# The first two query blocks of a head done at one point of the attention: 24 points in place of 32, in a decoder layer on one Trainium2 core

## The chip, the core and the metric

One core of a Trainium2 chip runs the whole layer in one launch. The metric is the device time of that launch in microseconds: the median of 3 runs of the kernel before is 610.11 us (609.85 to 610.28). The core has a matmul engine (PE, with PEld for its weight loads), a vector engine (DVE), a scalar engine (ACT), GpSimd (POOL) and SyncE (SP), each with its own list of instructions which it works off in order; they wait for each other by semaphores only. Most DMAs are issued from SP, the accumulating ones from POOL.

## The reference

One layer over 512 tokens of width 1024. A combined projection gives nine pieces of 1024 columns; two mixers, a gated MLP (branch A) and a differential attention (branch B), are merged and projected again, with a per-layer embedding and a LayerNorm at the end. The part that the change touches is the attention: 8 heads, two softmax maps each over 64-wide queries and keys, values of 128 columns.

```
h = x @ w_in
ua, va, za, qh, kh, vh, zb, ga, gb = jnp.split(h, IN_OFFSETS, axis=-1)
...
def block(args):                      # 128 queries, causal
    sc = jnp.einsum("bqhmd,bkhmd->bhmqk", qblk, k)
    sc = jnp.where(mask, sc, -jnp.inf)
    pr = jax.nn.softmax(sc, axis=-1)
    a = pr[:, :, 0] - lam * pr[:, :, 1]
    return jnp.einsum("bhqk,bkhd->bqhd", a.astype(v.dtype), v)
...
o = rms_norm(o, b_subln_g[i]) * (1.0 - lam_init)
yb = o.reshape(bn, s_len, B_WIDTH) * jax.nn.silu(zb)
```

## The kernel before, in words

All large products are done as three matmuls of a high and a low part (`three`, L279), each a 128x512 matmul; such a matmul is called a product here. Every product goes through `product` (L267), which counts it in `clock[0]` and then calls whatever has been put on an agenda with `later(n, fn)` for that count. So all side work is placed by hand, in units of products: it is written into the engines' lists between two products, and that decides the order on every engine. The matmuls that the side work itself issues are not counted.

The attention lies inside the stage that projects k, q, ua (three rounds of 144 products, `rope` and `ua_pair`) and za (192 products). Its softmax runs while these products run. For a head h and a block i of 128 queries (32 pairs in all) there are four steps, placed by `block` (L860) at points given by the table `starts`:

- `scores` (L763) at `starts[e]`, e = 4h+i: four matmuls of 128 queries by n = 128(i+1) keys into two `sc` banks of PSUM (L769), then on DVE the mask with a running minimum (L776), a small correction (L780), and on ACT the exponential with its sum (L782), once for each map.
- `combine` (L786) `COMBINE[i]` products later, on DVE: reciprocal, ratio, and the two maps joined (L790, L792, L794).
- `transposes` (L798) at `starts[e + 2]`: i+1 transposes on PE into the only `tr` bank, and one ACT copy out of it (`at`, L805).
- `values` (L808) at `starts[e + 3]`: i+1 matmuls into the head's `po` bank (L814), of which there is one.

At one point of `starts`, PE therefore gets values of block e-3, transposes of block e-2 and scores of block e, in this order, between two products. A head's four blocks start 13, 16, 20 and 23 products apart (`PERIOD`, L50; for the last two heads times 0.78), 72 products a head.

After a head's last values come `squares` (L818: DVE multiplies `po` into `on`, L823, and clamps it; ACT squares it), `norm` (L830: DVE sums, POOL takes the power, L840, L841), `scale` (POOL, L847), `gated` (DVE, L851) and `turned` (L853: four transposes of `on` on PE, L857, and an ACT copy). `TAIL` and `LAST_TAIL` give their distances in products from the last values. `on` has one buffer, `at` two (shared with the squares), `p0`/`p1` three, q, k and kx three each.

Of the weights, each 128x1024 unit (24 products) is split by ACT (`wh`, L389) and DVE (`wl`, L392) about three units before it is used, on the same lists as the attention's side work. `wr` buffers are asked for again by SP once `wl` is made.

Of the kernel before, what the change touches and what calls it, by code (L numbers as in the profile page):

```python
# [17 lines left out]
AF = mybir.ActivationFunctionType  # L18
OP = mybir.AluOpType
AX = mybir.AxisListType  # L20

P = 128
D = 1024
T = 512
KT = D // P
NT = T // P
NH = 8
DK = 64
# [18 lines left out]
SWAP = 290  # L47
BEGIN = 14
STRETCH = 0.78
PERIOD = (13, 16, 20, 23)  # L50
COMBINE = (10, 11, 13, 12)
LAST_TURNS = (14, 27, 45)
PAIR = 144
TAIL = (2, 14, 26, 44, 56)
LAST_TAIL = (2, 10, 20, 32, 42)
SILU = (122, 5)
NORM = (174, 224, 276, 326)
SPLITS = {'va': ((0, 10), (13, 16)), 'wb': ((4, 7), (13, 16)), '': ((0, 4), (6, 12))}
# [175 lines left out]
def hybrid_layer(ctx: ExitStack, tc: tile.TileContext, a, out: bass.AP):  # L234
    nc = tc.nc
    pe, dve, act, pool, sp = nc.tensor, nc.vector, nc.scalar, nc.gpsimd, nc.sync
# [9 lines left out]
    def pbank(tag, bufs):  # L246
        return psum.tile([P, T], F32, tag=tag, name=f"ps_{tag}", bufs=bufs)
# [150 lines left out]
    def next_unit(name):  # L398
        u = cursor[0]
        assert STEPS[u][0] == name, (STEPS[u][0], name)  # L400
        cursor[0] += 1
        for g in (prep(u), prep(u + 1), prep(u + 2)):
            run(g)
        if not pumping:
            for v in range(u + 3, u + 6):
                run(load(v))
        spread(u + 3)
        if name in EARLY_ASK:
            later(ASK, lambda: run(load(u + 6)))
        return split.pop(u)  # L410
# [67 lines left out]
    ident = consts.tile([P, P], F32, name="ident")  # L478
# [6 lines left out]
    mask = ap_.tile([P, T], F32, name="mask")  # L485
# [8 lines left out]
    cs = rp.tile([P, T], F32, name="cs")  # L494
# [87 lines left out]
    neglam = consts.tile([P, 1], F32, name="neglam")  # L582
# [44 lines left out]
    def quad(name, left, banks, place, done):  # L627
# [132 lines left out]

    todo = {}

    def scores(h, i):  # L763
        n = (i + 1) * P
        q, k0, k1 = stacks["q", h], stacks["k", h], stacks["kx", h]
        sc = [pbank("sc", 2) for _ in range(2)]
        for m in range(2):
            for o, kk in enumerate((k0, k1)):
                pe.matmul(sc[m][:, :n], q[:, m, i * P:(i + 1) * P], kk[:, m, :n],  # L769
                          start=o == 0, stop=o == 1)  # L770
        pr = [ap_.tile([P, T], F32, name=f"p{m}", tag=f"p{m}", bufs=3) for m in range(2)]
        if i == 0:
            todo["st", h] = small([P, NT, 4], "sth", 2)
        st = todo["st", h][:, i, :]
        for m in range(2):
            dve.tensor_tensor_reduce(out=pr[m][:, :n], in0=sc[m][:, :n], in1=mask[:, T - n:],  # L776
                                     scale=-(DK ** -0.5), scalar=3e38, op0=OP.add, op1=OP.min,
                                     accum_out=st[:, m:m + 1])
            if m == 0:
                dve.tensor_scalar(out=st[:, 0:1], in0=st[:, 0:1], scalar1=-math.log(T),  # L780
                                  scalar2=None, op0=OP.add)
            act.activation(pr[m][:, :n], pr[m][:, :n], AF.Exp, bias=st[:, m:m + 1], scale=-1.0,  # L782
                           accum_out=st[:, 2 + m:3 + m])
        todo[h, i] = pr, st

    def combine(h, i):  # L786
        n = (i + 1) * P
        pr, st = todo[h, i]
        r1 = small([P, 1], "r1")
        dve.reciprocal(out=r1, in_=st[:, 3:4])  # L790
        rho = small([P, 1], "rho")
        dve.tensor_scalar(out=rho, in0=r1, scalar1=st[:, 2:3], scalar2=neglam[:, 0:1],  # L792
                          op0=OP.mult, op1=OP.mult)
        dve.scalar_tensor_tensor(out=pr[0][:, :n], in0=pr[1][:, :n], scalar=rho[:, 0:1],  # L794
                                 in1=pr[0][:, :n], op0=OP.mult, op1=OP.add)
        todo[h, i] = pr[0]

    def transposes(h, i):  # L798
        n = (i + 1) * P
        ad = todo[h, i]  # L800
        tr = pbank("tr", 1)
        for j in range(i + 1):
            pe.transpose(tr[:, j * P:(j + 1) * P], ad[:, j * P:(j + 1) * P], ident)  # L803
        at = ap_.tile([P, T], F32, name="at", tag="at", bufs=2)
        act.activation(at[:, :n], tr[:, :n], AF.Copy)  # L805
        todo[h, i] = at

    def values(h, i):  # L808
        at = todo.pop((h, i))
        if i == 0:  # L810
            todo["po", h] = pbank("po", 1)
        po = todo["po", h]
        for j in range(i + 1):
            pe.matmul(po[:, i * P:(i + 1) * P], at[:, j * P:(j + 1) * P],  # L814
                      v[:, j, h * P:(h + 1) * P], start=j == 0, stop=j == i)


    def squares(h):  # L818
        po = todo.pop(("po", h))
# [37 lines left out]
            pe.transpose(tr[:, i * P:(i + 1) * P], on[:, i, :], ident)  # L857
        act.activation(yb[:, h, :], tr, AF.Copy, scale=g08[:, 0:1])

    def block(h, i, starts):  # L860
        e = NT * h + i
        later(starts[e], scores, h, i)
        later(starts[e] + COMBINE[i], combine, h, i)
        later(starts[e + 2], transposes, h, i)
        later(starts[e + 3], values, h, i)
        if i == NT - 1:
            tail = TAIL if h < 5 else LAST_TAIL
            for d, fn in zip(tail, (squares, norm, scale, gated)):
                later(starts[e + 3] + d, fn, h)

    def attention():
        starts = []
        for h in range(NH):
            stretch = 1.0 if h < NH - 2 else STRETCH
            at = PAIR * (h // 2) + BEGIN + h % 2 * sum(PERIOD) * stretch
            for n in PERIOD:
                starts.append(round(at))
                at += n * stretch
        starts += [starts[-1] + n for n in LAST_TURNS]
        for h in range(NH):  # L880
            for i in range(NT):
                block(h, i, starts)
        for h in range(NH - 1):
            later(starts[NT * h + 9], turned, h)
        later(starts[-1] + LAST_TAIL[4], turned, NH - 1)

    later(LAMBDAS[0], load_constants)
    for n, fn in zip(LAMBDAS[1:], (lam_dots, lam_exps, lam)):
# [57 lines left out]
    for k in range(KT):  # L946
        if k % 2 == 0:
            h, l = next_unit("kq")
# [423 lines left out]
    for those in ((0, 1), (2, 3)):  # L1372
        for k in range(KT):
# [9 lines left out]
            h, l = units[k // 2]  # L1383
            m = slice((k % 2) * T, (k % 2 + 1) * T)
# [9 lines left out]
    for t in range(NT):  # L1394
        ts = slice(t * P, (t + 1) * P)
        for i, (c0, c1) in enumerate(last_columns[t][1:], 1):
            for k in range(KT):
# [4 lines left out]
                h, l = units[k // 2]  # L1402
                m = slice((k % 2) * T + c0 - T, (k % 2) * T + c1 - T)
# [45 lines left out]
```

## Time and profile before

| | |
|---|---|
| median of 3 runs | 610.11 us (609.85 to 610.28) |
| the profiled execution | 610.13 us, of which the span from first to last instruction is 608.2 us |
| PE busy | 600.1 us, 99% of the span, 2880 records |
| PEld / DVE / ACT / POOL busy | 503.1 / 464.8 / 346.7 / 125.4 us |
| attention stage | about 117 to 307 us of the span |
| PE / DVE / ACT / POOL busy in 117 to 307 us | 190.0 / 154.2 / 112.2 / 56.9 us |
| granted TensorE clock | 0.997 over the span |

How to read it: times are us from the start of the span. A row of the timeline gives start, duration, engine, line of the kernel, operation, what it writes and reads, and a count where equal rows were merged; in brackets the idle time before it and what ended that. A matmul's end is modelled and overlaps the next one's start, so on PE the distance from one start to the next says what a matmul costs, not the duration shown. A row of the groups gives busy time, mean ns of one, and idle time before. L numbers are lines of the kernel before.

### The profile page before, as it was taken

What the parts mean: (1) busy time and instruction counts of PE and PEld (TensorE: products, weight loads), DVE (VectorE), ACT (ScalarE), POOL (GpSimd) and SP (SyncE); (2) the same over time, 40 slices, a digit from 0 to 9 for tenths busy, and PEclk for the clock granted to TensorE, in tenths of its full rate; (3) what the DMA queues carried; (4) which work ended last, traced back from release to release, by engine and by line L of the source; (5) the groups of instructions that cost most, each with busy time, mean ns of one, the idle gap of its engine ahead of it and who ended that gap; (6) DMA issues with size and microseconds to landing.
All of it is one profiled execution on the core that took longest, in us unless ns stands there. A gap on an engine that the chain in (4) does not pass through costs nothing.

```text
span 608.2 us, 8270 instructions
## 1 busy us (share of the span) xinstructions
PE 600.1 (99%) x2880; PEld 503.1 (83%) x2880; DVE 464.8 (76%) x770; ACT 346.7 (57%) x537; POOL 125.4 (21%) x133
## 2 busy tenths in 40 slices
PE   9999999999999999999999999999999999999995
PEld 6888888888888888888888888888888888888885
DVE  6995645588789789678965788779687887879476
ACT  6656475755745745746676666554776565555310
POOL 1234121041252432422110321331120011110011
PEclk9999999999999999999999999999999999999998
DMA  8689899697887896892579988976999578997002
GB/s 309 228 246 182 252 205 227 237 240 252 277 208 277 273 258 230 240 313 61 150 310 288 305 241 217 273 175 191 286 244 306 172 206 250 253 256 288 27 35 103
DMA packets 44541, 138.23 MB, mean 227 GB/s; under 512 B 5940, under 2 KB 7092, under 8 KB 44148
## 3 DMA queue, kind: packets, MB, share of 16 engines
q1 hardware_dynamic: 34436, 102.97, 46.8%
q0 software_dynamic: 9488, 34.35, 30.6%
q8 instruction: 22, 0.36, 0.2%
q10 hardware_dynamic: 576, 0.39, 0.2%
q14 instruction: 19, 0.16, 0.1%
HBM read 118.69 MB, written 29.49 MB: 244 GB/s over the span
## 4 chain that ended last, share of the span: by engine, by line
PE 98%; DVE 1%; DMA 0%; DVEq 0%; issue 0%
PE ps_pp L268 56%; PE ps_sc L268 22%; PE ps_tx L268 9%; PE ps_sc L769 3%; PE ps_po L814 3%; PE ps_tr L803 1%; PE ps_po L268 1%; PE ps_tr L268 1%; PE ps_tr L1133 1%; PE ps_po L1133 1%; PE ps_tx L857 1%; DMA xr<-in_xT 0%; PE ps_po L1319 0%; PE ps_tr L1319 0%; DVE base L1361 0%; DVE xl L295 0%
## 5 line engine op out<-in xcount | busy, mean ns | idle before, releaser
L392 DVE TENSOR_TENSOR wl<-wr,wh 128x1024 fp32r<-128x1024 f32 x133 | 165.4, 1250 | 36.7 <-ACT wh L389 36.5
L389 ACT ACTIVATE wh<-wr 128x1024 fp32r<-128x1024 f32 x133 | 139.4, 1054 | 68.7 <-PE ps_pp L268 20.5
L268 PE MATMUL ps_pp<-xh,wh 128*128 128x512 f32 x232 | 91.2, 394 | 0.0
L268 PE MATMUL ps_pp<-xh,wl 128*128 128x512 f32 x232 | 91.0, 393 | 0.0
L268 PE MATMUL ps_pp<-xl,wh 128*128 128x512 f32 x232 | 90.4, 391 | 0.1
L365 POOL DMA_DIRECT2D wr<-in_w x30 | 25.8, 872 | 153.6 <-DVE wl L392 150.6
L268 PE MATMUL ps_pp<-wl,xh 128*128 128x512 f32 (+1 forms) x148 | 56.9, 384 | 0.0
L268 PE MATMUL ps_pp<-wh,xl 128*128 128x512 f32 (+1 forms) x148 | 56.8, 384 | 0.0
L268 PE MATMUL ps_pp<-wh,xh 128*128 128x512 f32 (+1 forms) x148 | 56.7, 383 | 0.0
L782 ACT ACTIVATE p<-p,sth 128x128 f32<-128x128 f32 (+3 forms) x64 | 35.5, 556 | 28.2 <-DVE sth L780 28.0
L268 PEld LDWEIGHTS ps_pp<-xl,wh 128*128 128x128 f32 x232 | 43.6, 188 | 9.3 <-DVE xl L295 0.5
L268 PEld LDWEIGHTS ps_pp<-xh,wh 128*128 128x128 f32 x232 | 43.5, 188 | 9.0 <-ACT wh L294 0.6
L268 PEld LDWEIGHTS ps_pp<-xh,wl 128*128 128x128 f32 x232 | 43.6, 188 | 8.7
L776 DVE CUSTOM_DVE_ANT_0 p<-ps_sc,mask 128x128 f32<-128x128 f32 (+3 forms) x64 | 31.0, 484 | 19.3 <-PE ps_sc L769 19.1
L268 PE MATMUL ps_sc<-wl,xsh 128*128 128x512 f32 x88 | 34.5, 392 | 0.0
L268 PE MATMUL ps_sc<-wh,xsh 128*128 128x512 f32 x88 | 34.4, 390 | 0.0
L268 PE MATMUL ps_sc<-wh,xsl 128*128 128x512 f32 x88 | 34.3, 390 | 0.0
L805 ACT ACTIVATE at<-ps_tr 128x128 f32<-128x128 f32 (+3 forms) x32 | 13.9, 436 | 32.9 <-PE ps_tr L803 27.5
L715 POOL TENSOR_TENSOR hl<-m,hl 128x512 fp32r<-128x512 f32 x16 | 23.4, 1502 | 43.9 <-ACT hl L710 26.6
L268 PEld LDWEIGHTS ps_pp<-wl,xh 128*128 128x128 f32 x148 | 27.8, 188 | 5.4
L268 PEld LDWEIGHTS ps_pp<-wh,xh 128*128 128x128 f32 x148 | 27.8, 188 | 5.4
L268 PEld LDWEIGHTS ps_pp<-wh,xl 128*128 128x128 f32 x148 | 27.8, 188 | 5.4
(304 smaller groups left out, 1335.2 us busy)
## 6 DMA issues: line engine op xcount, KB each, us to landing
wr<-in_w SPq DMA_DIRECT2D x83, 512.0 KB, 5.2
wr<-in_w POOLq DMA_DIRECT2D x30, 512.0 KB, 6.7
wa<-in_w POOLq DMA_DIRECT2D x12, 512.0 KB, 6.2
k<-hl SPq DMA_DIRECT2D x16, 256.0 KB, 4.8
q<-hl SPq DMA_DIRECT2D x16, 256.0 KB, 3.9
ws_va<-in_w POOLq DMA_DIRECT2D x8, 512.0 KB, 9.8
wr<-ws_va SPq DMA_DIRECT2D x8, 512.0 KB, 4.7
kx<-hl SPq DMA_DIRECT2D x12, 256.0 KB, 4.5
```

Source lines behind the costliest of these rows:

```text
L268: pe.matmul(ps, s, m, start=start, stop=stop, skip_group_check=read_within)
L365: pool.dma_start(out=raw[u], in_=weights(STEPS[FOLLOWS[u]][1]), accum_op=OP.add)
L389: act.activation(h, raw[u], AF.Copy)
L392: dve.tensor_tensor(out=l, in0=raw[u], in1=h.bitcast(F32), op=OP.subtract)
L715: pool.tensor_tensor(out=hl[:, 3 - j, :], in0=m[2 * j], in1=hl[:, j, :].bitcast(F32), op=OP.subtract)
L769: pe.matmul(sc[m][:, :n], q[:, m, i * P:(i + 1) * P], kk[:, m, :n], start=o == 0, stop=o == 1)
L776: dve.tensor_tensor_reduce(out=pr[m][:, :n], in0=sc[m][:, :n], in1=mask[:, T - n:], scale=-(DK ** -0.5), scalar=3e38, op0=OP.add, op1=OP.m ...
L782: act.activation(pr[m][:, :n], pr[m][:, :n], AF.Exp, bias=st[:, m:m + 1], scale=-1.0, accum_out=st[:, 2 + m:3 + m])
L803: pe.transpose(tr[:, j * P:(j + 1) * P], ad[:, j * P:(j + 1) * P], ident)
L805: act.activation(at[:, :n], tr[:, :n], AF.Copy)
L814: pe.matmul(po[:, i * P:(i + 1) * P], at[:, j * P:(j + 1) * P], v[:, j, h * P:(h + 1) * P], start=j == 0, stop=j == i)
L1133: pe.matmul(sa[:, t * P:(t + 1) * P], va[:, t, g * P:(g + 1) * P], aux[0][:, 0, g, :], start=True, stop=True)
```

## The change

Blocks 0 and 1 of a head become one group. Their scores are written side by side into the same two `sc` banks (columns 0 to 128 and 128 to 384), and the two probability tiles, the `tr` bank and the `at` tile are shared in the same way; blocks 2 and 3 are groups of their own. So a head has three points, 24, 23 and 25 products apart (again 72), and `starts` has 24 of them and three behind. At the first group's point there are eight score matmuls, four passes of mask and minimum and four exponentials; its `combine` does both blocks, 15 products later; three transposes are copied by one ACT instruction of 384 columns where there were one of 128 and one of 256. Matmuls, DVE instructions and exponentials are as many as before, of the same sizes; ACT has eight copies fewer (471 instructions in the order in place of 479), PE 2768 matmuls in both.

The distances of the steps after a head's values change too, the shorter table is used from head 4 on in place of head 5, and `turned` moves from the second block's point of the next head but one to the second group's point of that head (for head 6 to the last of the three points behind).

```
-PERIOD = (13, 16, 20, 23)
-COMBINE = (10, 11, 13, 12)
+GROUPS = (((0, slice(0, 128)), (1, slice(128, 384))), ((2, slice(0, 384)),), ((3, slice(0, 512)),))
+PERIOD = (24, 23, 25)
+COMBINE = (15, 13, 12)
 LAST_TURNS = (14, 27, 45)
-TAIL = (2, 14, 26, 44, 56)
-LAST_TAIL = (2, 10, 20, 32, 42)
+TAIL = (2, 14, 24, 37)
+LATE_TAIL = (2, 10, 19, 29, 45)
...
+    def scores(h, g):
         q, k0, k1 = stacks["q", h], stacks["k", h], stacks["kx", h]
         sc = [pbank("sc", 2) for _ in range(2)]
...
+        for i, cs in GROUPS[g]:
+            for m in range(2):
+                for o, kk in enumerate((k0, k1)):
+                    pe.matmul(sc[m][:, cs], q[:, m, i * P:(i + 1) * P], kk[:, m, :cs.stop - cs.start],
+                              start=o == 0, stop=o == 1)
+        for i, cs in GROUPS[g]:
+            st = todo["st", h][:, i, :]
+            for m in range(2):
+                dve.tensor_tensor_reduce(out=pr[m][:, cs], in0=sc[m][:, cs], in1=mask[:, T - (cs.stop - cs.start):],
...
+    def transposes(h, g):
+        ad = todo[h, g]
         tr = pbank("tr", 1)
+        n = GROUPS[g][-1][1].stop
+        for c in range(0, n, P):
+            pe.transpose(tr[:, c:c + P], ad[:, c:c + P], ident)
         at = ap_.tile([P, T], F32, name="at", tag="at", bufs=2)
         act.activation(at[:, :n], tr[:, :n], AF.Copy)
...
+    def group(h, g, starts):
+        e = len(GROUPS) * h + g
+        later(starts[e], scores, h, g)
+        later(starts[e] + COMBINE[g], combine, h, g)
+        later(starts[e + 2], transposes, h, g)
+        later(starts[e + 3], values, h, g)
+        if g == len(GROUPS) - 1:
+            for d, fn in zip(TAIL if h < 4 else LATE_TAIL, (squares, norm, scale, gated)):
                 later(starts[e + 3] + d, fn, h)
...
-            later(starts[NT * h + 9], turned, h)
-        later(starts[-1] + LAST_TAIL[4], turned, NH - 1)
+            later(starts[3 * h + (7 if h < NH - 2 else 8)], turned, h)
+        later(starts[-1] + LATE_TAIL[4], turned, NH - 1)
```

On PE, the two points at which head 1's blocks 0 and 1 start. In the kernel before (L814 are values, L803 transposes, L769 scores, with products between the two points):

```order
L814 MATMUL ps_po<-v,at 128x128 x2
L803 MATMUL ps_tr<-ident,p_1167 128x128 x3
L769 MATMUL ps_sc<-k,q 128x128
L769 MATMUL ps_sc<-kx,q 128x128
L769 MATMUL ps_sc<-k,q 128x128
L769 MATMUL ps_sc<-kx,q 128x128
...
L814 MATMUL ps_po<-v,at 128x128 x3
L803 MATMUL ps_tr<-ident,p_1232 128x128 x4
L769 MATMUL ps_sc<-k,q 128x256
L769 MATMUL ps_sc<-kx,q 128x256
L769 MATMUL ps_sc<-k,q 128x256
L769 MATMUL ps_sc<-kx,q 128x256
```

In the changed kernel the first group's point (values are L819, transposes L806, scores L774):

```order
L819 MATMUL ps_po<-v,at 128x128 x3
L806 MATMUL ps_tr<-ident,p_1147 128x128 x3
L774 MATMUL ps_sc<-k,q 128x128
L774 MATMUL ps_sc<-kx,q 128x128
L774 MATMUL ps_sc<-k,q 128x128
L774 MATMUL ps_sc<-kx,q 128x128
L774 MATMUL ps_sc<-k,q 128x256
L774 MATMUL ps_sc<-kx,q 128x256
L774 MATMUL ps_sc<-k,q 128x256
L774 MATMUL ps_sc<-kx,q 128x256
```

The eight score matmuls stand together, and one run of products between them is gone; the values and transposes that stood at the second point stand at other points of the head.

On DVE, the place where head 6's output leaves the `po` bank that head 7 takes next (`on` 2880 before, 2870 after). In the kernel before:

```order
L776 ISA p1_2870,sth_2777<-ps_sc_2864,mask_110 128x384
L776 ISA sth_2777 128x1
L821 RECIPROCAL r0h_2878<-sth_2569 128x4
L823 TENSOR_TENSOR on_2880<-ps_po_2714,r0h_2878 128x512
L825 TENSOR_SCALAR on_2880<-on_2880 128x512
```

In the changed kernel:

```order
L779 ISA p0_2855,sth_2723<-ps_sc_2853,mask_110 128x512
L779 ISA sth_2723 128x1
L783 TENSOR_SCALAR sth_2723<-sth_2723 128x1
L779 ISA p1_2856,sth_2723<-ps_sc_2854,mask_110 128x512
L779 ISA sth_2723 128x1
L825 RECIPROCAL r0h_2868<-sth_2523 128x4
L827 TENSOR_TENSOR on_2870<-ps_po_2709,r0h_2868 128x512
L829 TENSOR_SCALAR on_2870<-on_2870 128x512
```

The read of `po` now stands behind the mask passes of 512 columns in place of 384; on PE, head 7's first values follow that point after 14 products, where there were 15.

On DVE, the end of head 7. In the kernel before:

```order
L839 TENSOR_SCALAR ss_3073<-ss_3073 128x4
L1024 TENSOR_TENSOR ua_1043<-ua_1043,sz_3087 128x512
L1016 TENSOR_TENSOR xt_2547<-xt_2547 128x2x256
L392 TENSOR_TENSOR wl_3092<-wr0_2963,wh_3091 128x1024
L851 TENSOR_TENSOR on_3058<-on_3058,yb_754 128x512
```

In the changed kernel:

```order
L843 TENSOR_SCALAR ss_3016<-ss_3016 128x4
L1027 TENSOR_TENSOR ua_1043<-ua_1043,sz_3031 128x512
L1019 TENSOR_TENSOR xt_2503<-xt_2503 128x2x256
L855 TENSOR_TENSOR on_3001<-on_3001,yb_754 128x512
L393 TENSOR_TENSOR wl_3036<-wr0_2904,wh_3035 128x1024
```

The last head's `gated` now stands in front of the weight split, not behind it.

More of the change, by code (lines that the diff above doesn't have):

```diff
@@ L761, in hybrid_layer @@
     todo = {}
-    def scores(h, i):
-        n = (i + 1) * P
+    def scores(h, g):
         q, k0, k1 = stacks["q", h], stacks["k", h], stacks["kx", h]
         sc = [pbank("sc", 2) for _ in range(2)]
[L767 to L770, printed above, removed]
         pr = [ap_.tile([P, T], F32, name=f"p{m}", tag=f"p{m}", bufs=3) for m in range(2)]
-        if i == 0:
+        if g == 0:
@@ L773, in scores @@
             todo["st", h] = small([P, NT, 4], "sth", 2)
[L774 to L796, printed above, removed]
@@ L798, in transposes @@
-    def transposes(h, i):
-        n = (i + 1) * P
-        ad = todo[h, i]
+        todo[h, g] = pr
+        for i, cs in GROUPS[g]:
[7 more added lines that the diff above has]
+                dve.tensor_tensor_reduce(out=pr[m][:, cs], in0=sc[m][:, cs], in1=mask[:, T - (cs.stop - cs.start):],
+                                         scale=-(DK ** -0.5), scalar=3e38, op0=OP.add, op1=OP.min,
+                                         accum_out=st[:, m:m + 1])
+                if m == 0:
+                    dve.tensor_scalar(out=st[:, 0:1], in0=st[:, 0:1], scalar1=-math.log(T),
+                                      scalar2=None, op0=OP.add)
+                act.activation(pr[m][:, cs], pr[m][:, cs], AF.Exp, bias=st[:, m:m + 1], scale=-1.0,
+                               accum_out=st[:, 2 + m:3 + m])
@@ new lines, in combine @@
+    def combine(h, g):
+        pr = todo[h, g]
+        for i, cs in GROUPS[g]:
+            st = todo["st", h][:, i, :]
+            r1 = small([P, 1], "r1")
+            dve.reciprocal(out=r1, in_=st[:, 3:4])
+            rho = small([P, 1], "rho")
+            dve.tensor_scalar(out=rho, in0=r1, scalar1=st[:, 2:3], scalar2=neglam[:, 0:1],
+                              op0=OP.mult, op1=OP.mult)
+            dve.scalar_tensor_tensor(out=pr[0][:, cs], in0=pr[1][:, cs], scalar=rho[:, 0:1],
+                                     in1=pr[0][:, cs], op0=OP.mult, op1=OP.add)
+        todo[h, g] = pr[0]
@@ L801, in transposes @@
+    def transposes(h, g):
+        ad = todo[h, g]
         tr = pbank("tr", 1)
-        for j in range(i + 1):
-            pe.transpose(tr[:, j * P:(j + 1) * P], ad[:, j * P:(j + 1) * P], ident)
+        n = GROUPS[g][-1][1].stop
+        for c in range(0, n, P):
+            pe.transpose(tr[:, c:c + P], ad[:, c:c + P], ident)
         at = ap_.tile([P, T], F32, name="at", tag="at", bufs=2)
         act.activation(at[:, :n], tr[:, :n], AF.Copy)
[L806 to L810, printed above, removed]
+        todo[h, g] = at
@@ L811, in values @@
+    def values(h, g):
+        at = todo.pop((h, g))
+        if g == 0:
             todo["po", h] = pbank("po", 1)
         po = todo["po", h]
-        for j in range(i + 1):
-            pe.matmul(po[:, i * P:(i + 1) * P], at[:, j * P:(j + 1) * P],
-                      v[:, j, h * P:(h + 1) * P], start=j == 0, stop=j == i)
+        for i, cs in GROUPS[g]:
+            for j in range(i + 1):
+                c = cs.start + j * P
+                pe.matmul(po[:, i * P:(i + 1) * P], at[:, c:c + P], v[:, j, h * P:(h + 1) * P],
+                          start=j == 0, stop=j == i)
@@ L858, in turned @@
         act.activation(yb[:, h, :], tr, AF.Copy, scale=g08[:, 0:1])
[L860 to L868, printed above, removed]
+    def group(h, g, starts):
[6 more added lines that the diff above has]
+            for d, fn in zip(TAIL if h < 4 else LATE_TAIL, (squares, norm, scale, gated)):
                 later(starts[e + 3] + d, fn, h)
@@ L880, in attention @@
         for h in range(NH):
-            for i in range(NT):
-                block(h, i, starts)
+            for g in range(len(GROUPS)):
+                group(h, g, starts)
         for h in range(NH - 1):
-            later(starts[NT * h + 9], turned, h)
-        later(starts[-1] + LAST_TAIL[4], turned, NH - 1)
+            later(starts[3 * h + (7 if h < NH - 2 else 8)], turned, h)
+        later(starts[-1] + LATE_TAIL[4], turned, NH - 1)
     later(LAMBDAS[0], load_constants)
```

## The prediction

> **What bounds the kernel now.** I read the page's busy times, then the waits of PE, then the attention stage alone, then PE start by start. From the page the line of busy times; from the waits of PE the only row there is; from the stretches the attention stage (PE, PEld, DVE, ACT, POOL busy, clock, DMA share, GB/s).
>
> ```profile
> PE 600.1 (99%) x2880; PEld 503.1 (83%) x2880; DVE 464.8 (76%) x770; ACT 346.7 (57%) x537; POOL 125.4 (21%) x133
> PE ps_po L462 <- DVE zeros L459: 1.3, 1, 1.3
> 117.00:307.00 190.00, 190.00 (x1013) 163.76 (x1013) 154.16 (x397) 112.19 (x242) 56.88 (x54) 1.00 0.77 232
> ```
>
> PE is the bound and nothing else is: it waited once, for 1.3 us, at the very start, and in the 190 us of the attention stage it is busy throughout at full clock, while DVE has 36 us free and ACT 78 us. So the change can gain only what PE itself spends on having 32 points rather than 24, and can lose only by a wait that PE does not have today. What DVE, ACT and the queues save is hidden by PE, whatever it is.
>
> A busy PE could still lose time where it goes from products to small matmuls and back, since its ends are modelled. The starts tell. Here are head 0's blocks 0 and 1 on PE, which the change puts together, from the timeline of PE:
>
> ```profile
> 117.05 0.22 PE L769 MATMUL ps_sc<-k,q 128*128 128x128 f32 x1
> 117.10 0.28 PE L769 MATMUL ps_sc<-kx,q 128*128 128x128 f32 x1
> 117.22 0.27 PE L769 MATMUL ps_sc<-k,q 128*128 128x128 f32 x1
> 117.33 0.27 PE L769 MATMUL ps_sc<-kx,q 128*128 128x128 f32 x1
> 117.44 0.45 PE L268 MATMUL ps_pp<-xh,wl 128*128 128x512 f32 x1
> 117.72 0.40 PE L268 MATMUL ps_pp<-xh,wh 128*128 128x512 f32 x1
> 117.96 0.39 PE L268 MATMUL ps_pp<-xl,wh 128*128 128x512 f32 x1
> ...
> 120.45 0.28 PE L769 MATMUL ps_sc<-k,q 128*128 128x256 f32 x1
> ...
> 121.39 0.39 PE L268 MATMUL ps_pp<-xh,wl 128*128 128x512 f32 x1
> ```
>
> From 117.96 to 120.45 lie eleven products, 2.49 us: a product costs 0.2265 us from start to start. From the first small matmul at 117.05 to 117.96 there are four of 128 columns and two products: 0.91 less 0.453 leaves 0.457 us, 0.114 each. From 120.45 to 121.39 there are four of 256 and two products: 0.94 less 0.453 leaves 0.487 us, 0.122 each. The visible sign of a switch is the product at 117.44, which takes 0.28 us to the next start in place of 0.227; but the first small matmul took only 0.05, so most of that is given back.
>
> A later point has values and transposes in front of the scores (head 2's block 0):
>
> ```profile
> 158.84 0.60 PE L814 MATMUL ps_po<-v,at 128*128 128x128 f32 x4
> 159.28 0.49 PE L803 MATMUL ps_tr<-ident,p 128*128 128x128 f32 x3
> 159.53 0.31 PE L769 MATMUL ps_sc<-k,q 128*128 128x128 f32 x1
> ...
> 160.53 0.39 PE L268 MATMUL ps_pp<-xl,wh 128*128 128x512 f32 x1
> ```
>
> Four value records take 0.44 (0.11 each); three transposes 0.25 where three times 0.11 would be 0.33; the scores and two products 1.00 where head 0 needed 0.91. So 0.08 early and 0.09 late: the switch from transposes to scores costs about 0.01 us.
>
> **The change part by part.** *PE.* Matmuls, their sizes and their total are unchanged. What goes are 8 stretches of products between two points, and with each one entry into small matmuls and one return to products. The return costs at most what the two rows behind 117.44 show above a product, 0.05 and 0.01 us, less what the first small matmul gave back. Put together, head 0's two blocks would take the four of 128 (0.39 to 117.44), the same late step of 0.05, then the four of 256 (0.487), 0.93 us in place of 0.944. With the 0.01 at the transposes a point costs between 0.01 and 0.02 us; 8 of them **0.1 us**. The bounds: if nothing that looks early is really given back, 0.09 + 0.06 = 0.15 us a point, 1.2 us gained; if the first 256-column matmul behind the 128-column ones is late by the 0.09 that scores behind transposes show, and nothing is early for it, 8 x 0.09 = 0.7 us lost. I take 0.1, which is nearest to the whole rows (start of the first small matmul to the settled product), since those contain both the late and the early step.
>
> *ACT, DVE, POOL, SP.* Eight ACT copies fewer, with as many exponentials: hidden under PE, 0. DVE issues the same instructions; four mask passes now come in a row, and `combine` waits for four exponentials. Behind that wait stand weight splits; each is placed 14 products into a unit for the third unit behind it, 58 products or 13 us ahead of its use, so a wait of 1 or 2 us costs nothing; without that cover it would cost its length on PE. No moved step issues a DMA. The last scores of a head come 2 products earlier (47 in place of 49), so q, k and kx buffers come free earlier for SP; block 1's scores come 14 products or so earlier than now, but read the tiles that block 0's already read.
>
> *Handovers to PE.* For most of them the distance grows: from one point to the next, which is from scores to the next scores in the same banks and from transposes to their values, it is 23 to 25 products in place of 13 to 23. Two get tighter or were tight. The first is the `po` bank from head 6 to head 7. The rows, from the timelines of PE and DVE: scores of 512 columns, their mask passes, then `on` read from `po` and head 7's first values:
>
> ```profile
> 152.61 0.47 PE L769 MATMUL ps_sc<-k,q 128*128 128x512 f32 x1
> 153.38 0.40 PE L769 MATMUL ps_sc<-kx,q 128*128 128x512 f32 x1
> 153.62 0.39 PE L268 MATMUL ps_pp<-xh,wh 128*128 128x512 f32 x1
> ...
> 154.60 0.68 DVE L776 CUSTOM_DVE_ANT_0 p<-ps_sc,mask 128x512 f32<-128x512 f32 x1
> 156.01 0.08 DVE L776 DVE_READ_ACCUMULATOR2_ANT sth<- 128x1 f32 x1
> ...
> 280.05 0.18 DVE L821 RECIPROCAL r0h<-sth 128x4 f32<-128x4 f32 x1
> 280.26 0.69 DVE L823 TENSOR_TENSOR on<-ps_po,r0h 128x512 f32<-128x512 f32 x1
> ...
> 282.50 0.27 PE L814 MATMUL ps_po<-v,at 128*128 128x128 f32 x1
> ```
>
> Today `on` is done at 280.95 and head 7's values start at 282.50: 1.55 us to spare. In the changed order PE has the four scores (1.01) and 14 products (3.17), 4.18 us from the first score to the values. DVE can start once the first two scores are done, by the fourth's start at the latest (0.77), then needs 1.49 for the two passes (154.60 to 156.09) and 0.90 for reciprocal and `on` (280.05 to 280.95): 3.16. It keeps 1.0 us to spare; cost 0, and up to 0.5 us if DVE comes to the scores 1.5 us late.
>
> The second is head 7's end, where the last four transposes stand between za and va with nothing else to fill PE (timelines of POOL, DVE and PE, and L840's eight durations, min, median and max in ns):
>
> ```profile
> 301.74 1.45 POOL L840 TENSOR_TENSOR f<-ss,mhalf 128x4 f32<-128x4 f32 x1 [13.87 <-DVE ss L839]
> ...
> 305.25 0.69 DVE L851 TENSOR_TENSOR on<-on,yb 128x512 f32<-128x512 f32 x1 [1.22 <-POOL on L847]
> 306.22 0.60 PE L857 MATMUL ps_tr<-ident,on 128*128 128x128 f32 x4
> L840 POOL TENSOR_TENSOR f<-ss,mhalf x8: 1032/1948/1994, 153.6 to 301.7; 128x4 f32<-128x4 f32 x8
> ```
>
> Between the end of `gated` (305.94) and the transposes 0.28 us is all there is. In the new order head 7's last point is one product (0.23) earlier, and head 6's four transposes (some 0.36, as three took 0.25) stand right behind its values, not earlier in the stage, so PE comes to that point 0.36 earlier; `on`, which has one buffer, can be written again 0.36 later against the point, once they have read it. Together the chain starts about 0.2 us earlier against PE's end of the stage. `gated` no longer stands behind a weight split. I cost it at 0; if POOL's power takes 1.99 in place of 1.45, PE waits 0.1 to 0.3 us.
>
> *The sum.* The profiled execution took 610.13 us, 1.93 more than its span of 608.2. PE -0.1, handovers 0: span 608.1, execution 610.03. That execution lies 0.02 above the median of 610.11, so the median becomes 610.0.
>
> **The rivals.** *Each point empties PE's pipeline* (faster). If what the first small matmul and the last transpose seem to give back is only the model of the records, a point costs 0.15 us and the 8 are worth 1.2: 608.9. For it speaks the late product at 117.44; against it that the whole runs add up to 0.114 us a matmul of 128 columns, beside 0.11 for values and transposes, with nothing left over. The Trainium skill, TensorE: Matmul & The Clock Gate, section Single matmul latency, gives a lone matmul some 166 ns beyond its columns, which a stream hides; by that page an emptied pipeline at each of 8 points would be an estimated 1.3 us. The trace does not show such an emptying at any point here.
>
> *The doubled burst on DVE holds back `gated`* (slower). DVE works in order, so what the first group adds at one point stands in front of other heads' steps: two more passes of 256 columns with their sums, a second `combine`, and a wait for four exponentials in place of two. The rows of the passes, of `combine`'s join, of DVE's waits for exponentials (total, times, longest), and of head 6's `gated` with the transposes behind it:
>
> ```profile
> L776 DVE CUSTOM_DVE_ANT_0 p<-ps_sc,mask 128x256 f32<-128x256 f32 x16 | 6.7, 418 | 2.0 <-PE ps_sc L769 1.7
> L794 DVE SCALAR_TENSOR_TENSOR p<-p,rho,p 128x256 f32<-128x256 f32 x8 | 3.9, 485 | 0.3
> DVE r L790 <- ACT p L782: 8.7, 14, 1.0
> 289.86 0.69 DVE L851 TENSOR_TENSOR on<-on,yb 128x512 f32<-128x512 f32 x1
> 291.90 0.27 PE L857 MATMUL ps_tx<-ident,on 128*128 128x128 f32 x1
> ```
>
> Two passes with their sums are 2 x (0.42 + 0.08) = 1.0 us, the join 0.49, a wait like the longest 1.0: 2.5 us. Between the end of `gated` and the transposes lie 1.35 us today, so a `gated` that slides by all of it makes PE wait 1.15 us; in the three heads whose distances are cut for the short table, 4 to 6, that is 3.4 us: 613.4. It decides from a slide of 1.35 us on. Against it: in the first four heads `gated` stands 12 products behind the first group's point and 3 ahead of its `combine`, so that half of the burst is behind it and the other long done, and 12 products are still to come before the transposes; in head 5, where these are 9, they were 11. The Trainium skill, on the same page, section Architectural detail, states that ACT's and DVE's queues are strictly first in, first out, which speaks against putting four exponentials into one wait. The trace agrees in the 1.0 us that DVE stood before L790; by that rule alone, with nothing to spare, it would be the 613.4 above.
>
> *A handover at the end of the stage waits* (within the bound): 0.3 to 0.8 us at `po` or head 7's end, 610.3 to 610.8.
>
> **How the numbers follow.** A measurement of this kernel can tell about 0.2% from no change, 1.2 us. The forecast, no wait and 0.1 us gained, 0.72: 610.0. A handover that waits, 0.15, still the same. The emptied pipeline, 0.04, at 608.9 and beyond: faster. The burst on DVE, 0.09: slower. So same 0.87, faster 0.04, slower 0.09. The range takes in half of the gain that PE's bounds allow (609.3) and PE's bound of loss or a waiting handover (611.0); about 0.15 lies outside.
>
> **What would show it.** Right: PE's only wait remains the one at the start; between two points products still start 0.2265 us apart; a first group's eight scores and two products take about 0.09 + 0.93 + 0.453, 1.47 us, from the first score behind transposes to the third product; ACT has eight copies fewer and more idle time, and PE's last start comes 0.1 us earlier. Wrong: a start distance on PE of 0.5 us and more ahead of values or of the transposes of `on` (a handover or the burst), a weight split used less than 1 us after it is made, or points whose eight matmuls take less than 0.8 us.

## The result, and the profile after

| | before | changed |
|---|---|---|
| median | 610.28 us (609.72 to 611.05, 21 runs) | 611.37 us (610.64 to 614.0, 21 runs) |
| span of the profiled execution | 608.2 us | 609.4 us |
| PE waits after the start | none | 1.1 us, and one of 0.23 us that only the start distances show |

The ratio is 1.002 (95% interval 1.0014 to 1.0026): 1.1 us slower, just outside the predicted range of 609.3 to 611.0, where 610.0 was forecast.

PE's waits in the changed kernel: the one at the start that was there before, and a new one, for a DMA. (In the changed kernel scores are L774, the q load is L732; lines up to L760 are one higher than before.)

```profile
PE ps_po L463 <- DVE zeros L460: 1.3, 1, 1.3
PE ps_sc L774 <- DMA q<-hl: 1.1, 1, 1.1
```

It lies at head 6's first point, between the scores of the first map and those of the second (timeline of PE):

```profile
249.89 0.49 PE L806 MATMUL ps_tr<-ident,p 128*128 128x128 f32 x3
250.14 0.30 PE L774 MATMUL ps_sc<-k,q 128*128 128x128 f32 x1
250.28 0.27 PE L774 MATMUL ps_sc<-kx,q 128*128 128x128 f32 x1
251.62 0.30 PE L774 MATMUL ps_sc<-k,q 128*128 128x128 f32 x1 [1.07 <-DMA q<-hl]
```

From 250.28 to 251.62 PE starts nothing: 1.34 us where 0.11 is normal, a loss of 1.23 us. Head 6's q comes in two loads, one for each map. These are the tile q's rows on when they are issued and how long they take to land, before and changed:

```profile
L731 SPq DMA_DIRECT2D q<-hl x2: 536/566/595, 244.0 to 244.6; - x2
DMA to landing us min/median/max: 2.4/2.4/2.4
```

```profile
L732 SPq DMA_DIRECT2D q<-hl x2: 536/566/596, 242.9 to 243.5; - x2
...
DMA to landing us min/median/max: 2.7/5.4/8.0
```

Before, both took 2.4 us and the second landed at 247.1, 3.6 us before PE asked for it at 250.69. In the changed kernel they are issued 1.1 us *earlier*, and the second takes 8.0 us. What the DMA engines did meanwhile, in the two microseconds from 246 to 248 of the changed kernel:

```profile
DMA packets 75, 0.31 MB, mean 154 GB/s; under 512 B 0, under 2 KB 0, under 8 KB 75
## 3 DMA queue, kind: packets, MB, share of 16 engines
q0 software_dynamic: 75, 0.31, 94.3%
```

Nothing but packets of the software queue, POOL's. Why they are there is in the timelines of POOL, before and changed:

```profile
241.13 2.86 POOL L715 TENSOR_TENSOR hl<-m,hl 128x512 fp32r<-128x512 f32 x2 [11.98 <-ACT hl L710]
244.51 1.95 POOL L840 TENSOR_TENSOR f<-ss,mhalf 128x4 f32<-128x4 f32 x1 [0.51 <-DVE ss L839]
246.54 0.20 POOL L841 TENSOR_TENSOR f<-f,ok 128x4 f32<-128x4 f32 x1
246.82 1.04 POOL L847 TENSOR_TENSOR on<-on,f 128x512 f32<-128x512 f32 x1
247.80 1.75 POOL L324 DMA_DIRECT2D ws_pg<-in_w  x2
```

```profile
240.32 2.53 POOL L716 TENSOR_TENSOR hl<-m,hl 128x512 fp32r<-128x512 f32 x2 [9.06 <-ACT hl L711]
242.79 0.86 POOL L325 DMA_DIRECT2D ws_pg<-in_w  x1
249.34 1.03 POOL L844 TENSOR_TENSOR f<-ss,mhalf 128x4 f32<-128x4 f32 x1 [5.70 <-DVE r L793]
```

`hl` is what q is loaded from, so q's load is issued as soon as POOL is done with it. Behind it in POOL's list stood, before, head 4's norm and scale, and then two accumulating transfers of 512 KB for pg (`make_sums`). Those transfers are due at a fixed count of products, the first at 430; head 4's norm, which hangs on the attention's points, was due at 417 and is now due at 431. So the first transfer has overtaken the norm by one count, and goes out at 242.79, just ahead of q at 242.87 and 243.5, in place of 247.80, when q had landed.

The second, smaller loss stands at the end of the stage, where the prediction had 0.28 us of slack (timelines of POOL, DVE and PE, changed kernel):

```profile
292.07 1.33 POOL L851 TENSOR_TENSOR on<-on,f 128x512 f32<-128x512 f32 x1
303.68 1.41 POOL L844 TENSOR_TENSOR f<-ss,mhalf 128x4 f32<-128x4 f32 x1 [10.28 <-DVE ss L843]
```

```profile
291.83 2.12 DVE L1019 TENSOR_TENSOR xt<-xt 128x512 f32<-128x512 f32 x1
...
298.63 0.68 DVE L1027 TENSOR_TENSOR ua<-ua,sz 128x512 f32<-128x512 f32 x1
299.23 0.17 DVE L825 RECIPROCAL r0h<-sth 128x4 f32<-128x4 f32 x1
...
306.52 0.69 DVE L855 TENSOR_TENSOR on<-on,yb 128x512 f32<-128x512 f32 x1 [1.73 <-POOL on L851]
```

```profile
296.69 1.05 PE L819 MATMUL ps_po<-v,at 128*128 128x128 f32 x8
...
306.91 0.39 PE L269 MATMUL ps_pp<-xh,wl 128*128 128x512 f32 x1
307.36 0.63 PE L861 MATMUL ps_tr<-ident,on 128*128 128x128 f32 x4
```

The last product and the transposes are 0.45 us apart, 0.23 more than a product takes. POOL's power took 1.41, no longer than before, so that is not the cause. DVE came late to head 7's squares: it started them at 299.23 without a pause, 1.5 us after PE had finished the values (296.69 and 1.05). In the kernel before it stood waiting for PE at that place:

```profile
297.56 0.69 DVE L823 TENSOR_TENSOR on<-ps_po,r0h 128x512 f32<-128x512 f32 x1 [0.20 <-PE ps_po L814]
```

One pass, `xt` at 291.83, took 2.12 us where others of its kind take 0.68. Beside it POOL ran head 6's scale. Before, the scale (at 285.76, 1.32 us) stood beside a weight split on DVE:

```profile
285.82 2.35 DVE L392 TENSOR_TENSOR wl<-wr,wh 128x1024 fp32r<-128x1024 f32 x1
```

Such splits take 1.22 us elsewhere, so DVE lost 1.1 us there too. But before it came to the squares it was idle twice, for 0.66 us and 0.20 us. In the changed kernel the delay comes 6 us later, and no idle time follows it before the squares.

What the points themselves did shows in the stage as a whole. From the 481st product to the 1151st, PE has the same 1071 records in both kernels (windows; before, then changed; the columns are the window, its length, the busy time of PE, PEld, DVE, ACT and POOL, the clock, the DMA share and GB/s):

```profile
113.87:317.11 203.24, 203.24 (x1071) 174.72 (x1070) 162.75 (x407) 124.37 (x258) 56.88 (x54) 1.00 0.77 238
```

```profile
113.83:318.30 204.47, 203.34 (x1071) 174.46 (x1070) 160.46 (x407) 123.23 (x250) 51.48 (x54) 1.00 0.78 237
```

The stage is 1.23 us longer. The two waits add 1.46, so without them it would be 0.23 us shorter than before. The end of head 0's first group:

```profile
117.80 0.28 PE L774 MATMUL ps_sc<-kx,q 128*128 128x256 f32 x1
117.92 0.40 PE L269 MATMUL ps_pp<-xh,wl 128*128 128x512 f32 x1
118.16 0.40 PE L269 MATMUL ps_pp<-xh,wh 128*128 128x512 f32 x1
```

Before, the product behind four scores of 128 columns took 0.28 us to the next start (117.44 to 117.72). Here a product stands behind scores of 256 columns and takes 0.24.

### The profile page after: what moved, and what is told of

It reads as the page before. It is cut to its first block, busy times and chain, and to the rows that moved or that the text cites. A ratio compares the mean times of both kernels' runs of the same rounds, so it can differ in the third digit from the quotient of the medians.

```text
span 609.4 us, 8250 instructions
## 1 busy us (share of the span) xinstructions
PE 600.2 (99%) x2880; PEld 503.0 (83%) x2880; DVE 462.4 (76%) x770; ACT 344.6 (57%) x529; POOL 120.0 (20%) x133
## 4 chain that ended last, share of the span: by engine, by line
PE 94%; DMA 3%; DVE 1%; issue 1%; POOL 0%; SPq 0%; DVEq 0%; POOLq 0%
PE ps_pp L269 52%; PE ps_sc L269 22%; PE ps_tx L269 9%; PE ps_sc L774 3%; PE ps_po L819 2%; DMA q<-hl 1%; PE ps_tr L806 1%; DMA ws_wb<-ws_wb 1%; PE ps_po L269 1%; PE ps_tr L269 1%; DMA kx<-hl 1%; PE ps_po L463 1%; PE ps_tr L1136 1%; PE ps_po L1136 1%; PE ps_tx L861 0%
## 5 line engine op out<-in xcount | busy, mean ns | idle before, releaser
L808 ACT ACTIVATE at<-ps_tr 128x384 f32<-128x384 f32 (+1 forms) x24 | 12.7, 528 | 40.1 <-PE ps_tr L806 37.5
```

## The experiments

Two theories at first. *The transfer*: POOL's accumulating transfer, overtaking head 4's norm, holds q back. *The order*: the loss lies in the moved points themselves (eight scores at once, PE earlier at head 6, DVE's burst), and the late q goes with it. The ratios are to the kernel before as timed in the same session (610.30 us for e1 to e4, 610.59 for e5 to e8, 610.52 for e9 and e10).

**e1_pg_later.** The changed kernel with pg's accumulating transfers 22 counts later, behind head 4's norm and scale.

```
-'pg': (320, 430)
+'pg': (320, 452)
```

> The changed kernel with one entry of a table altered: the accumulating transfers for pg, which POOL issues at products 430 and 442, come at 452 and 464, behind head 4's scale. Collision theory (the second half of head 6's q load queues on the DMA engines behind the first of these transfers, which POOL now issues about 5 us earlier than in the kernel before): the q load lands within 3 us of its issue, PE's 1.2 us wait before head 6's first scores is gone, only the 0.23 us before the last transposes is left, span about 608.2, time 610.2 to 610.4. Rival (the grouping itself: q lands late because PE comes to head 6's first scores 0.8 us earlier, or for SP's own loads): the wait stays at 0.8 to 1.2 us, time 611.2 to 611.5.

610.26 us (ratio 0.9998, 0.9989 to 1.0007). q's halves take 2.4 us again, POOL issues the transfers at 252.2, and the wait is gone; what is left on PE is the 0.23 us at the end, in a stage of 203.15 us.

**e4_pg_sooner.** The same transfers 44 counts sooner.

```
-'pg': (320, 430)
+'pg': (320, 386)
```

> The changed kernel with the transfers for pg at products 386 and 398, ahead of the subtraction that makes q, so that they are over or nearly so when q is loaded. Collision theory: no wait or a short one at head 6 (below 0.3 us), 610.2 to 610.6, unless the transfers hold back POOL's subtraction, which the trace would show as a later issue of q. Rival (the grouping): wait 0.8 to 1.2 us, 611.2 to 611.5.

610.47 us (ratio 1.0, 0.9991 to 1.0009). POOL issues them at 231.8, 13 us ahead of q, and PE does not wait for q. On either side of q the transfers cost nothing: only their place beside the load does.

**e2_before_pg_earlier.** The kernel before, with the transfers moved to the place that the changed kernel gave them.

```
-'pg': (320, 430)
+'pg': (320, 411)
```

> The kernel before, 32 points and its own tables, with the accumulating transfers for pg at products 411 and 423 in place of 430 and 442, so that POOL issues the first one right behind the subtraction that makes q, as in the changed kernel. Collision theory: the second half of head 6's q load lands 7 to 8 us after its issue in place of 2.5, and PE, which comes to these scores 0.8 us later than in the changed kernel, waits 0.4 to 1 us there: 610.6 to 611.3. Rival (the grouping): no wait, 610.1 to 610.4 as before.

614.89 us (ratio 1.0072, 1.0057 to 1.0087): the loss appears without the change, and larger than expected. Both transfers went early here (the second at 247.19), and the wait is 3.0 us (PE waits):

```profile
PE ps_sc L769 <- DMA q<-hl: 3.0, 1, 3.0
```

It has a second part, in the windows of PE a microsecond after the wait:

```profile
255.20:258.00 2.80, 2.80 (x8) 2.20 (x7) 2.21 (x5) 0.29 (x2) 0.00 (x0) 0.50 1.08 247
```

The granted clock is 0.50, and seven products take 0.427 us each in place of 0.2265, another 1.4 us.

**e7_before_one_early.** To take one transfer alone: only the first is early, as in the changed kernel.

```
-    later(at[i] + APART * j, step, n, what, of, j)
+    later(at[i] + (31 if name == "pg" and i else APART) * j, step, n, what, of, j)
```

with pg's count 411 as in e2_before_pg_earlier.

> The kernel before, with only the first of pg's two accumulating transfers 19 products earlier, so that POOL issues it just ahead of head 6's q, as in the changed kernel; the second one stays at its count (in e2_before_pg_earlier both were moved, and head 6's first scores waited 3.0 us). Theory: one such transfer holds the second half of q back by itself: it lands some 8 to 9 us after POOL's issue, at 252 to 253.5 in place of 247.1, and PE, which asks for it at 250.6, waits 1.5 to 2.7 us: median 611.8 to 613.0. No products at half clock as in e2_before_pg_earlier (seven of 0.427 us there), if these come from the length of the wait. Rival: one transfer alone does nothing in the old order (610.3), and the changed order of points is needed for the loss.

613.70 us (ratio 1.0047, 1.0034 to 1.0061). One transfer is enough, in the old order: the second half of q takes 8.5 us, PE waits 2.4 us.

```profile
PE ps_sc L769 <- DMA q<-hl: 2.4, 1, 2.4
```

```profile
253.76:257.20 3.44, 3.44 (x11) 2.70 (x10) 2.74 (x7) 0.49 (x2) 0.00 (x0) 0.51 1.10 280
```

The wait is in the expected range. The median is above it, because the expectation that no product would be slow was wrong: eight of them run at half clock after 2.4 us, as seven did after 3.0. By the mean clocks this does not happen every time. Of the five executions here one has a mean granted clock of 0.997, as the kernel before has (0.996 to 0.999), and is 2.4 us over it, about the wait alone; the other four have 0.994 and 0.995 and are 2.9 to 4.0 us over. In e2_before_pg_earlier two of six have 0.997, at 3.1 and 3.2 us over, and four 0.995.

**e6_point_later.** The changed kernel with head 6's first point 4 products later; the transfer stays.

```
+        starts[18] += 4
```

> The changed kernel, with head 6's first point (its eight scores, and the values and transposes of head 5 that stand there) put 4 products later, 0.91 us. Theory: the wait at head 6's first scores is the landing of the second half of q minus the time at which PE asks for it, and the landing does not move, because POOL's accumulating transfer is still issued just ahead of q. The wait shrinks from 1.1 to 0.2 us, the stall of 1.34 us between two scores to 0.4, and the median falls from 611.37 to 610.5. Rival: the loss lies in the moved order itself (eight scores at one point, DVE's double burst) and q's late half is only beside it: then the median stays at 611.2 to 611.5, or a wait of the same length shows at another step.

610.82 us (ratio 1.0, 0.9991 to 1.0009), somewhat above the 610.5 expected; the wait falls from 1.1 to 0.3 us while q's second half still takes 8.2 us:

```profile
PE ps_sc L774 <- DMA q<-hl: 0.3, 1, 0.3
```

So the loss is q's landing less the time at which PE asks for it, and 0.9 us more in front of the question takes off 0.8 us of it. The moved order brought PE to this point only 0.3 us earlier than before (250.39 for 250.69 at the third score), so it made up a quarter of the wait at most.

**e8_split_add.** The changed kernel with the first transfer, at its place, in two halves.

```
-    pool.dma_start(out=there[n, j], in_=source, accum_op=OP.add, max_dma_last_dim=4096)
+    for c in (slice(0, 512), slice(512, 1024)) if name == "pg" and j == 0 else (slice(0, 1024),):
+        pool.dma_start(out=there[n, j][:, c], in_=source[:, c], accum_op=OP.add, max_dma_last_dim=4096)
```

> The changed kernel, with pg's first accumulating transfer issued as two of 512 columns, one behind the other, in place of one of 1024; bytes and place are the same. Theory: the 16 DMA engines work off one accumulating transfer whole before the packets of a load that was issued after it, so the second half of q, issued between the two, waits for one half only: it lands at 248.5 to 250 in place of 251.5, the PE wait is gone and the median is 610.3. Rival: while any accumulating transfer is under way the load gets nothing, whatever the cut: the second half lands at 251.5 or later (packets half as long, twice as many, and one issue of 0.86 us more), the wait stays at 1.1 us or grows, median 611.4 to 612.

610.54 us (ratio 0.9992, 0.9984 to 1.0001). The bytes are the same. The first half is still issued in front of q (242.73, q at 242.83 and 243.42), the second beside q's second load (243.35). That load takes 5.9 us in place of 8.0, and PE does not wait for it. From 246 to 248 packets of both queues now run (tile q, then the DMA queues):

```profile
DMA to landing us min/median/max: 2.8/4.3/5.9
```

```profile
q0 software_dynamic: 104, 0.18, 75.4%
q1 hardware_dynamic: 107, 0.20, 26.6%
```

So the load is held up by the whole of the transfer issued ahead of it, not by accumulating traffic as such: the second half is still under way when q lands. (The edit also halves the rows of that transfer, to 2048 bytes; no run separates the two.) The Trainium skill, DMA: Bandwidth & Descriptors, section Queues, rings and completion order, says that each DMA engine takes turns between its queues, and drains a whole packet of several descriptors, typically 9 to 17, before it switches. The trace agrees: 128 rows of 4096 bytes on 16 engines are 8 an engine, and no packet of a load runs beside them from 246 to 248 in the changed kernel, where 107 do here.

With the q wait explained, the 0.23 us at the end were open. *The buffer*: head 6's four transposes, moved, free `on` late. *DVE*: it is behind when it comes to head 7's squares.

**e3_turned6_earlier.** The changed kernel with those four transposes 10 products earlier.

```
-    later(starts[3 * h + (7 if h < NH - 2 else 8)], turned, h)
+    later(starts[3 * h + 7] + (0 if h < NH - 2 else 8), turned, h)
```

> The changed kernel with head 6's transposes 10 products earlier (574 in place of 584), so that they no longer stand between head 7's last values and the reuse of the tile on. Theory on the small wait: it is this reuse that made the last chain late, so the 0.23 us before the last transposes goes and the 1.2 us at head 6 stays: 611.1, 0.2 to 0.3 under the changed kernel. Rival (POOL's power and product take longer): 0.2 us stays, 611.3 to 611.4.

613.12 us (ratio 1.0047, 1.0035 to 1.0059). The 0.23 us are gone, but the edit brought a wait of its own, and after the stage one of 0.5 us for a weight split:

```profile
PE ps_tx L861 <- DVE on L855: 1.8, 1, 1.8
```

A PE that stands for 1.8 us gives DVE time to catch up, so this run does not tell the two apart; e5_piece_later does.

**e5_piece_later.** e1_pg_later, with one pass of DVE (a sister of `xt`, 0.68 us) taken from in front of head 7's squares.

```
-    later(XS[2] + XS[3] * (2 * i + kp), add_x, kp, c)
+    later(XS[2] + XS[3] * (2 * i + kp) + (18 if 2 * i + kp == 5 else 0), add_x, kp, c)
```

> The kernel of the run e1_pg_later, with one more edit: one of the eight xt pieces on DVE (the sixth, 0.68 us) stands behind head 7's row sums in place of ahead of head 7's squares. Theory: the 0.23 us that PE still waits ahead of head 7's last transposes comes from DVE, which reaches head 7's squares 1.3 us after PE has finished the values, without a pause before them. Taking 0.6 us of other work from in front of the squares moves the whole chain 0.6 us forward and the wait is gone: PE then waits nowhere after the start, the span is 0.2 to 0.3 us below that of e1_pg_later at equal begin (608.5, so 608.2 to 608.3), the median 610.0. Rival: the wait comes from the buffer of on, which head 6's four transposes free late; then the squares cannot start earlier, the wait stays at 0.23 us and the median at 610.26.

610.01 us (ratio 0.9989, 0.998 to 0.9998). `on`'s buffer is freed where it was, and the wait is gone: it was DVE. PE waits nowhere after the start, and the stage is shorter than before:

```profile
113.79:316.68 202.89, 202.89 (x1071) 174.47 (x1070) 159.46 (x407) 123.10 (x250) 51.46 (x54) 1.00 0.78 238
```

**e9_scale_on_dve.** Why DVE was behind: e1_pg_later with head 6's scale on DVE in place of POOL.

```
-    pool.tensor_tensor(out=on, ...)
+    (dve if h == 6 else pool).tensor_tensor(out=on, ...)
```

> The kernel of the run e1_pg_later, with head 6's scale on DVE in place of POOL. Theory: DVE comes late to head 7's squares because one of its passes of 512 columns (xt, 291.03 us, 2.13 us in place of 0.68) stands still while POOL's scale of 1.33 us runs beside it. On DVE the scale costs 0.6 to 0.7 us, but xt is back at 0.68: DVE reaches head 7's squares 0.7 to 0.9 us earlier, PE's wait of 0.23 us ahead of the last transposes is gone, stage from product 480 to product 1150 some 202.9 us in place of 203.15, median 610.0. Rival: xt is long for another reason (POOL's DMA issue of 0.89 us just ahead, or the transfers that write its tile); then xt stays above 1.5 us, DVE is later by the scale, and PE waits 0.5 us or more.

609.78 us (ratio 0.999, 0.998 to 0.9999), stage 202.89. DVE has one pass more and is done earlier:

```profile
290.17 0.69 DVE L851 TENSOR_TENSOR on<-on,f 128x512 f32<-128x512 f32 x1 [0.27 <-POOL f L845]
290.78 0.68 DVE L1027 TENSOR_TENSOR ua<-ua,z 128x512 f32<-128x512 f32 x1
291.38 0.69 DVE L1019 TENSOR_TENSOR xt<-xt 128x512 f32<-128x512 f32 x1
...
297.48 0.18 DVE L825 RECIPROCAL r0h<-sth 128x4 f32<-128x4 f32 x1
```

`xt` is back at 0.69 and the squares start at 297.48 where e1_pg_later had 298.42: 0.94 us earlier, 0.7 of it against PE, whose stage began 0.24 sooner. POOL still issues a transfer beside these passes (0.89 us from 290.39), so it was the scale that had held `xt`. The Trainium skill, SBUF — State Buffer, section SBUF: two separate sides, says that DVE and POOL share one pair of ports, which whoever starts first keeps for the whole instruction, against a DVE pass with two inputs in SBUF too. `xt` is such a pass; its 2.12 us are 0.68 and some 1.4, about the 1.33 of the scale beside it. The trace agrees that the two do not run together, but not on who keeps the ports: by the records `xt` started 0.24 us ahead of the scale (291.83 and 292.07), and was the one held.

**e10_sixteen_more_points.** Last, the price of a point: e5_piece_later with 16 more of them, the second map's scores one product behind the first's in the second and third groups.

```
+        later(1, rest, h, g, sc) if g else rest(h, g, sc)
```

where `rest` holds the second map's two score matmuls and everything behind them.

> The kernel of the run e5_piece_later, in which in the second and third group of every head the two score matmuls of the second map come one product after those of the first map: 16 more entries into small matmuls and returns to products, the same matmuls. Theory, from the stage from product 480 to product 1150, which is 203.24 us before and 202.89 in e5_piece_later with 8 points fewer and no wait in either: a point costs PE 0.04 us, so the stage grows by 0.7 us, to 203.6, and the median to 610.7. Rival, the price of the prediction: a point costs 0.01 us, the stage grows by 0.1 to 0.2 us, to 203.05, and the 0.35 us have another source. A handover that gets one product tighter could add a wait of up to 0.3 us, which would show as a stall of its own.

610.20 us (ratio 0.9997, 0.9985 to 1.0009), stage 202.97, no wait. Sixteen more points cost 0.08 us, 0.005 each, the prediction's kind of price and not the 0.04 that e5_piece_later seemed to show. But these points split scores only; none of them has values or transposes in front, as seven of the 8 that went had.

So where the 0.35 us lie has to be read from the starts. Summed over the stage, the distances from a product to the next start are 0.82 us less in e5_piece_later than before (153.33 us for 154.16, 670 products in both), and those from a small matmul are 0.47 us more (49.56 for 49.08). Of the 0.82, 0.39 is the product behind a first block: before, eight products stood behind four scores of 128 columns and took 0.284 us to the next start, and in the changed kernel the product stands behind scores of 256 columns and takes 0.235; 8 x 0.049 is 0.39. The other 0.47 us are mostly transposes, with 0.57 more: the last transpose of a point takes 0.028 us to the next start where the others take 0.109, and there were 31 such last ones and are 24. The other small matmuls together come 0.10 us cheaper. No run changed one of these alone.

## Why the prediction was wrong

*The failed step* is "ACT, DVE, POOL, SP", and in it "No moved step issues a DMA", with its cost of 0. The sentence is true, and the wrong question. Head 4's norm and scale on POOL issue nothing; but they stood in front of a transfer that does, and when they moved the transfer was free to go. I looked at q's load only for its buffers. The queue that a moved step leaves has to be read like the one that it joins: what comes next in it, and what that meets. It cost 1.23 us (e1_pg_later, e4_pg_sooner), more than everything else together. POOL's own list in the two orders shows it without a run.

*PE*: -0.1 us was forecast and -0.35 measured (203.24 to 202.89, e5_piece_later and e9_scale_on_dve). Right in sign and within the bounds; mis-sized is the price of a point, 0.01 to 0.02 us forecast and 0.044 for the 8 that went. It is a difference of two terms, as forecast, but the return to products was worth 0.10 us a point (0.82 over the stage) where the two rows behind 117.44 gave 0.06 at most, and 0.06 (0.47) was given back. "The same late step of 0.05", which I let stay when the two blocks are put together, went. That alone does not explain it: the first group takes 1.46 us from the first score behind transposes to the third product, and 1.47 was forecast, so most of the surplus lies outside the group, in rows that head 0 does not show.

*The `po` bank*: 1.0 us to spare forecast. `on` was read at 286.36 and head 7's values started at 287.51, 1.15 us. Right.

*Head 7's end*: cost 0, "if POOL's power takes 1.99 in place of 1.45, PE waits 0.1 to 0.3 us". PE waits 0.23, but for another reason: the power took 1.41, and DVE started the chain late. "Together the chain starts about 0.2 us earlier" counted the products and `on`, not whether DVE had time. The cause is again a moved POOL step: head 6's scale, which cost DVE about as much before, now beside a pass with no idle time behind it.

*The sum*: -0.35 + 1.23 + 0.23 is 1.11 us; the stage measured 1.23 and the medians 1.09. The 0.12 us between sum and stage are spread over many starts, and I do not place them.

*The rivals*: the emptied pipeline, 0.15 us a point, is not borne out by the 0.044 of the 8 points or the 0.005 of e10_sixteen_more_points. The burst on DVE did not hold back `gated`: the transposes of no head before the last waited. "A handover at the end of the stage waits" came true at 0.23 us, a little under its 0.3 to 0.8, by a cause it did not name: that is luck. What the slower side would look like I had tied to DVE; no rival was on a DMA, though q's load has a landing time that could be read off the trace, with 3.6 us of slack.

The two cures, e5_piece_later and e9_scale_on_dve, measure 0.1% below the kernel before (0.998 to 0.9998, and 0.998 to 0.9999), at the edge of what these runs resolve. On PE the change is worth 0.35 us, by the stage in both, once what it had let loose is put back in its place.

## What to carry to other kernels

When steps move, read the list of each engine that they leave: an instruction behind them now goes sooner, and if it is a DMA, ask which load is issued within a few microseconds of it and how much slack that load has. Where a small load that PE waits for shares the DMA engines with large accumulating transfers, put these well ahead or behind, or cut them. And a pass on POOL can take time on DVE too (1.1 us from the split, 1.4 from `xt`): where DVE has no idle time before a handover, the POOL step beside it belongs in the sum.

## What was not expected of the hardware

A 256 KB load that takes 2.4 us alone took 8.0 to 8.5 us behind one accumulating transfer of 512 KB issued 0.7 us before it, and 5.9 us when that transfer was cut in two. The load of q's first map, issued within 0.1 us of the transfer, took 2.7 to 2.8.

PE's clock fell to half after a wait of 2.4 us (eight products of 0.427 us, e7_before_one_early) and of 3.0 us (seven, e2_before_pg_earlier), by the mean clocks in most executions of these two but not in all. It did not after 1.1 us in the changed kernel, nor after 1.8 us in e3_turned6_earlier (mean clock 0.997 to 0.999 in all five). The Trainium skill, TensorE: Matmul & The Clock Gate, section What's actually happening, gives an idle window of about 3.4 us before the clock drops; here a shorter stop was enough, and the measurement decides.

POOL's power of 128x4 elements took 1.95 to 1.99 us in five of eight heads before and 1.01 to 1.05 us in six of eight in the changed kernel, on the same line with the same shape. The rows beside it tell them apart. Each of the five started 0.14 to 0.18 us after a weight split on DVE, as the row at 244.51 did:

```profile
244.37 1.22 DVE L392 TENSOR_TENSOR wl<-wr,wh 128x1024 fp32r<-128x1024 f32 x1
```

So did the one long power of the changed kernel (1.94 us, at 269.93), and none of the short ones stands beside a split. The last head's 1.45 and 1.41 us stand behind the start of a `ua` pass of 0.69 us. So a DVE pass seems to hold POOL up as the scale held `xt`; no run moved a split away from a power to show it.
